# A Mamba-2 mixer with one decay matrix for both directions, and a reordered front, in a two-stream trunk layer

## The chip, the cores and the metric

The kernel runs on one core of a Trainium2 chip. The metric is the device time of one execution in microseconds. The engines are named as the profile names them: PE (TensorE), DVE (VectorE), ACT (ScalarE), POOL (GpSimd) and SP (the engine whose queue issues most of the DMAs; ACT's queue issues some).

## The reference

One layer of a hybrid trunk is computed for 256 context tokens and 1024 latent tokens, with a model width of 1024, all in float32:

```python
shift1, scale1, gate1, shift2, scale2, gate2 = split(silu(c) @ ada_w + ada_b, 6)
h = rmsnorm(x, norm1_g) * (1 + scale1) + shift1
proj = h @ w_in
y_ssd = ssd_mixer(proj[..., :OFF_SGU]);  y_sgu = sgu_mixer(...);  y_s5 = s5_mixer(...)
x = x + gate1 * (concatenate([y_ssd, y_sgu, y_s5]) @ w_out)
h = rmsnorm(x, norm2_g) * (1 + scale2) + shift2
x = x + gate2 * (square(relu(h @ ffn_w1)) @ ffn_w2)
...
# SSD, in each of two directions, per chunk of 128 tokens and head (the backward one on flipped tokens):
seg = a_cum[q] - a_cum[k];  lmat = exp(where(lower, seg, -inf))
y_diag = (C B^T * lmat) @ (x * dt)
chunk_state = B^T @ (decay_to_end * dt * x);  h = chunk_decay * h + chunk_state
y_off = (C @ h_prev) * exp(a_cum)
y = y_f + flip(y_b) + D * x
```

A final rmsnorm follows. The S5 mixer is a complex diagonal scan over 16 groups of 64 states, and the gating mixer (SGU) works on blocks of 128 tokens.

## The kernel before

Matrix products keep float32 accuracy by splitting each operand into a high and a low part and adding three products (`mm3`, lines 219 to 221). Most activations stand with channels on partitions and tokens along the free axis. The tokens are held as three tiles of 256, 512 and 512 columns (`hi[t]`, `lo[t]`), and the first norm works on five blocks of 256 tokens.

The program is written as one long sequence; the order in which each engine really gets its instructions is made by a planner, which simulates the program and puts instructions of later parts into gaps of earlier ones. Each engine, and each queue that issues DMAs, then works strictly in that order. Tiles come from rings with a fixed number of buffers (`bufs`), and a tile waits until the one that used its buffer last has been read.

The part of the program ahead of the second norm, which we call the front, runs in this order:

- The modulation that the first norm needs (`ada_norm1`, four column groups of `ada_w`), the S5 tables (`s5_tables`, mostly small POOL and DVE work), and the weights of the first projections.
- Per block of 256 tokens: load x by channels (`x_block`), `x_stats` (four ACT squares, POOL sums in pairs, then eight matmuls against a column of ones, line 200, the square root and reciprocal, a broadcast by two matmuls, line 205, and an ACT copy `r` to SBUF, line 267), then `x_norm`: for each of eight channel groups one DVE scale `x<-x,gs,r`, one ACT shift that also rounds to `hi`, and one DVE `lo`.
- `vdt` (value half of the SGU and the time steps) per 128 tokens, `s5_in_tile` per token tile, and `s5_prep` for eight pairs of S5 groups, which makes tables on POOL and DVE, transposes and multiplies some on PE, and stores them to DRAM on ACT's queue. `s5_in_store` writes the S5 inputs to `u5_d` with 16 DMAs on the same queue, and `s5_taps` writes its filter taps with eight DMAs for each half.
- `sgu_mix`, then `s5_main` for eight pairs of groups: it reads u, M, Y, XT and Et back on SP's queue, two scans on DVE, products on POOL.
- Four `xbc_slab`s (projection, depthwise convolution, SiLU), `dt_chain`, and two `u_slab`s.
- The SSD (`ssd_group`, twice, for four heads each). For each of ten chunks `outputs()` loads the rows of cumulated decay `rb` (broadcast to all partitions, 512 KB), makes one matrix exp(min(...)) in `rb[:, 1]`, multiplies it by C·B under either triangular mask (line 886: `rb[:, 0]` on DVE, `rb[:, 1]` on POOL), makes `xd`, x times dt for both directions, and adds in PSUM: D times x through a diagonal matrix `diagd` (line 893) and, for both directions and four heads, `xd` times `rb` (line 896). The state's share `po` (line 903) is scaled and added behind it. `new_state` carries the state on.
- In the loops over chunks stand also the other 64 steps of the modulation (`adaln`, line 170: each loads 256 KB of `ada_w` and does four small matmuls), the z slabs, `s5_glu`, and the gathering of mixed outputs (`mixed_tile`) with the first output slabs.

Then come the output projection, the second norm and the feed-forward part, which fill the rest of the time and which the diff does not touch.

## Time and profile before

| | |
|---|---|
| runs | 1589.42, 1590.81, 1593.71 us; median 1590.81 us |
| the profiled execution | 1586.03 us, span from first to last instruction 1584.2 us |
| mean granted TensorE clock | 0.954 of 2.4 GHz |
| busy share of the span | PE 92%, DVE 68%, ACT 46%, POOL 28% |
| matmuls | 8664 records (a float32 matmul that is not split leaves two) |
| first feed-forward matmul | near 708 us |

The span is the time between the first and the last instruction in one execution; the profiled execution's own time is 1.8 us more than its span. Busy times are sums of the recorded durations with overlaps counted once. Matmuls overlap in the pipeline, so the record of one can be longer than the time that it takes from the next.

### The profile page before, as it was taken

To read this page: it belongs to the slowest core of one execution; us is meant where nothing else is said; L and a number is where in the kernel's file an instruction comes from. 1 tells how busy PE (TensorE), PEld (TensorE's weight loads), DVE (VectorE), ACT (ScalarE), POOL (GpSimd) and SP (SyncE) were. 2 spreads that over 40 slices of the span, in tenths; PEclk is the share of its full clock that TensorE was granted. 3 is DMA by queue.
4 is the path that set the end of the run, shared out by engine and by line. 5 is a ranking of instruction groups with operands and counts; after the bars stand their busy time and mean duration, and the time that the engine had idled before them with its cause. 6 is when DMAs were issued, how large, how long until landed. Compare 5 with 4: busy or idle time off the path is not lost.

```text
span 1584.2 us, 24203 instructions
## 1 busy us (share of the span) xinstructions
PE 1459.8 (92%) x8664; PEld 1226.9 (77%) x8664; DVE 1075.9 (68%) x1807; ACT 723.0 (46%) x1428; POOL 447.5 (28%) x537
## 2 busy tenths in 40 slices
PE   4789988999897889989999999999899999999895
PEld 4677877877674668878888888888788988887795
DVE  5885587575755665558977765674554768979945
ACT  3565534463533533436655554455646333424322
POOL 4875376624333331321100000000240313032023
PEclk9699999999997889999999999999999999999897
DMA  9414546368778677446444443444844245415302
GB/s 325 141 68 135 179 149 192 86 182 216 208 261 210 204 246 235 121 123 192 130 156 150 149 141 116 137 140 141 264 132 161 67 160 171 123 54 180 113 34 100
DMA packets 238808, 249.12 MB, mean 157 GB/s; under 512 B 15808, under 2 KB 165344, under 8 KB 238688
## 3 DMA queue, kind: packets, MB, share of 16 engines
q1 hardware_dynamic: 222592, 230.32, 46.9%
q10 hardware_dynamic: 16096, 17.27, 3.2%
q8 instruction: 68, 1.11, 0.3%
q14 instruction: 52, 0.43, 0.1%
HBM read 178.63 MB, written 68.89 MB: 156 GB/s over the span
## 4 chain that ended last, share of the span: by engine, by line
PE 59%; DVE 8%; DMA 6%; issue 2%; ACT 2%; POOL 1%; SPq 0%; DVEq 0%; ACTq 0%; POOLq 0%
PE ps_w L1193 7%; PE ps_w L1194 7%; PE ps_w L1192 7%; PE ps_w L1349 6%; PE ps_w L1348 6%; PE ps_w L1350 6%; PE ps_mm L221 4%; PE ps_mm L219 4%; PE ps_mm L220 4%; DMA xc<-xbc_d 2%; DVE X L54 2%; PE ps_mm L1350 1%; PE ps_mm L1349 1%; PE ps_mm L1348 1%; DMA rb<-rows_d 1%
## 5 line engine op out<-in xcount | busy, mean ns | idle before, releaser
L219 PE MATMUL ps_mm<-hi,wh 128*128 128x512 f32 (+1 forms) x576 | 211.8, 368 | 6.4 <-DVE dtr L686 2.8
L221 PE MATMUL ps_mm<-hi,wl 128*128 128x512 f32 (+1 forms) x576 | 209.4, 364 | 0.9 <-DVE wl L54 0.9
L220 PE MATMUL ps_mm<-lo,wh 128*128 128x512 f32 (+1 forms) x576 | 209.8, 364 | 0.2 <-DVE lo L54 0.2
L1348 PE MATMUL ps_w<-uB,uA 128*128 128x512 f32 (+1 forms) x520 | 190.7, 371 | 9.3 <-ACT uB L60 8.9
L1349 PE MATMUL ps_w<-uB,uA 128*128 128x512 f32 (+1 forms) x520 | 191.7, 369 | 7.7 <-DVE uB L54 7.7
L1350 PE MATMUL ps_w<-uB,uA 128*128 128x512 f32 (+1 forms) x520 | 190.5, 367 | 0.0
L54 POOL TENSOR_TENSOR cb<-h 128x512 f32<-128x512 f32 x14 | 21.1, 1512 | 512.5 <-DMA h<-w 402.7
L219 PEld LDWEIGHTS ps_mm<-hi,wh 128*128 128x128 f32 x576 | 111.2, 193 | 24.7 <-DVE dtr L686 3.2
L221 PEld LDWEIGHTS ps_mm<-hi,wl 128*128 128x128 f32 x576 | 110.9, 193 | 19.1 <-issue 2.4
L220 PEld LDWEIGHTS ps_mm<-lo,wh 128*128 128x128 f32 x576 | 111.1, 193 | 15.9 <-issue 1.2
L1348 PEld LDWEIGHTS ps_w<-uB,uA 128*128 128x128 f32 x520 | 99.9, 193 | 25.4 <-ACT uB L60 9.3
L1349 PEld LDWEIGHTS ps_w<-uB,uA 128*128 128x128 f32 x520 | 100.1, 192 | 24.5 <-DVE uB L54 9.6
L1350 PEld LDWEIGHTS ps_w<-uB,uA 128*128 128x128 f32 x520 | 100.0, 192 | 15.4
L54 DVE TENSOR_TENSOR uB<-tb,uB 128x512 fp32r<-128x512 f32 x106 | 88.7, 857 | 13.5 <-ACT uB L60 13.5
L60 ACT ACTIVATE uB<-tb 128x512 fp32r<-128x512 f32 x106 | 65.6, 625 | 62.1 <-PE ps_w L1350 31.7
L54 DVE TENSOR_TENSOR wl<-wraw,wh 128x1024 fp32r<-128x1024 f32 x32 | 50.3, 1572 | 40.6 <-ACT wh L60 40.2
L54 DVE TENSOR_TENSOR X<-X,ps_w 128x512 f32<-128x512 f32 x84 | 56.1, 680 | 27.7 <-PE ps_w L1350 27.6
L54 DVE TENSOR_TENSOR q<-q,ps_w 128x512 f32<-128x512 f32 x48 | 32.9, 686 | 60.2 <-PE ps_w L1194 59.5
L60 ACT ACTIVATE c<-c 128x512 f32<-128x512 f32 x64 | 40.3, 629 | 56.9 <-DVE c L54 55.9
L54 POOL TENSOR_TENSOR sq<-sq 128x512 f32<-128x512 f32 (+1 forms) x31 | 41.1, 1331 | 81.8 <-ACT sq L60 81.3
L1350 PE MATMUL ps_mm<-ch,uA 128*128 128x256 f32 x224 | 63.2, 283 | 0.0
L1349 PE MATMUL ps_mm<-cl,uA 128*128 128x256 f32 x224 | 63.2, 283 | 0.0
(430 smaller groups left out, 3993.9 us busy)
## 6 DMA issues: line engine op xcount, KB each, us to landing
rw<-w SPq DMA_DIRECT2D x112, 256.0 KB
tb<-a_d SPq DMA_DIRECT2D x106, 256.0 KB
aw<-ada_w SPq DMA_DIRECT2D x64, 256.0 KB
h<-w SPq DMA_DIRECT2D x32, 512.0 KB
a_d<-t SPq DMA_DIRECT2D x42, 256.0 KB
rb<-rows_d SPq DMA_DIRECT2D x20, 512.0 KB
adaw<-ada_w SPq DMA_DIRECT2D x32, 256.0 KB
wraw<-w_out SPq DMA_DIRECT2D x16, 512.0 KB
```

Source lines behind the costliest of these rows:

```text
L54: eng.tensor_tensor(out=out, in0=a, in1=b, op=op)
L60: S.activation(out=out, in_=in_, func=func, **kw)
L219: T.matmul(out, lhsT=wh(k), rhs=xh(k), start=(k == 0), stop=False)
L220: T.matmul(out, lhsT=wh(k), rhs=xl(k), start=False, stop=False)
L221: T.matmul(out, lhsT=wl(k), rhs=xh(k), start=False, stop=(k == nk - 1))
L1192: T.matmul(out, lhsT=wh, rhs=X[0][:, j, :], start=(j == 0), stop=False)
L1193: T.matmul(out, lhsT=wh, rhs=X[1][:, j, :], start=False, stop=False)
L1194: T.matmul(out, lhsT=wl, rhs=X[0][:, j, :], start=False, stop=(j == 3))
L1348: T.matmul(out, lhsT=wh, rhs=bh, start=start, stop=False)
L1349: T.matmul(out, lhsT=wh, rhs=bl, start=False, stop=False)
L1350: T.matmul(out, lhsT=wl, rhs=bh, start=False, stop=stop)
```

## The change

Four things are altered.

- **The SSD chunk.** The two masked products are combined into one matrix, since both directions share C·B and exp(min(...)): for each head, ACT writes `cm[:, 0]` times dt of the forward direction into `rb[:, 0]`, DVE adds `cm[:, 1]` times dt of the backward one, and a single DVE product makes `rb[:, 1]`. The matmul with x itself (`xs`, an ACT copy) then covers both directions: four matmuls instead of eight. D times x leaves PE (`diagd` goes away) and becomes two DVE instructions with `dcol`. `wdec` is multiplied by dt for both directions, so that `new_state` can start from x in PSUM, on DVE for both. The ring of `xc` gets five buffers instead of three.
- **Squares by tokens.** For blocks 1 to 4, `x_rms` replaces `x_stats`: it loads the same x a second time with tokens on partitions (a new input array `xN`, four DMAs of 256 KB a block), lets ACT's squares add up along the row, and leaves the broadcast factor in PSUM, where `x_norm` reads it.
- **Order.** `s5_prep`, in steps, moves from between the norms to between the projections; the two `u_slab`s move ahead of the last steps of it; the 64 modulation steps move from the SSD loops to the projections (five groups of eight) and to `s5_main` (three groups), with their tiles in the common ring `ev`.
- **S5 arrays in DRAM.** `u5_d`, `y5_d` and `kt_d` are stored by channel. The writes of u and of the taps become one DMA in place of eight, the reads in `s5_glu` one in place of eight; the reads and the write of `s5_main` (u2, M, y2) become two in place of one.

```diff
     m5_d = dram.tile([256, NT], F32, name="m5_d")
-    u5_d = dram.tile([16, 8, 16, JP], F32, name="u5_d")
-    y5_d = dram.tile([16, 8, 16, 161], F32, name="y5_d")
-    kt_d = dram.tile([16, 8, 16, 128], F32, name="kt_d")
+    u5_d = dram.tile([256, 8, JP], F32, name="u5_d")
+    y5_d = dram.tile([256, 8, 161], F32, name="y5_d")
+    kt_d = dram.tile([256, 8, 128], F32, name="kt_d")
     yc_d = dram.tile([8, 128, 576], F32, name="yc_d")
...
         return r
+    def x_rms(i):
+        t, o = BLK[i]
+        c0 = TILES[t][0] + o
+        ss = cst.tile([128, 2, 2], F32, tag="ss", name="ss", bufs=2)
+        for j in range(2):
+            for a in range(2):
+                xn = ev("xn")
+                load(xn, I["xN"][c0 + j * 128:c0 + (j + 1) * 128, a * 512:(a + 1) * 512])
+                act(xn, xn, ACT.Square, accum_out=ss[:, j, a:a + 1])
+        rt = cst.tile([128, 4], F32, tag="rt", name="rt", bufs=3)[:, 0:2]
+        tt(rt, ss[:, :, 0], ss[:, :, 1], ALU.add)
+        rstd(rt, rt, D)
+        p = bank("w", 5)
+        for j in range(2):
+            T.matmul(p[:, j * 128:(j + 1) * 128], lhsT=rt[:, j:j + 1].to_broadcast([128, 128]), rhs=ident,
+                     start=True, stop=True)
+        return p[:, 0:256]
...
         tt(kt[:, 112:128], kt[:, 112:128], pk[:, 240:256], ALU.add)
-        for tau in range(8):
-            load(kt_d[hf * 8:(hf + 1) * 8, tau].rearrange("g c n -> g c n"), kt[:, (7 - tau) * 16:(7 - tau) * 16 + 128], nc.scalar)
+        win = bass.AP(kt.tensor, kt.offset + 112, [kt.ap[0], [-16, 8], [1, 128]])
+        load(kt_d[hf * 128:(hf + 1) * 128], win, nc.scalar)
...
     def s5_in_store(m, us):
-        for tau in range(8):
-            load(u5_d[m * 8:(m + 1) * 8, tau], us[:, tau, :], nc.scalar)
+        load(u5_d[m * 128:(m + 1) * 128], us, nc.scalar)
...
         u2 = pool.tile([128, 2, JP], F32, tag="u2", name="u2", bufs=3)
-        load(u2, u5_d[gp * 2:gp * 2 + 2].rearrange("g t c j -> (t c) g j"))
+        gs = [slice((gp * 2 + i) * 16, (gp * 2 + i + 1) * 16) for i in range(2)]
+        for i in range(2):
+            load(u2[:, i, :], u5_d[gs[i]].rearrange("c t j -> t c j"))
         M = pool.tile([128, 2, 128], F32, tag="M", name="M", bufs=3)
-        load(M, kt_d[gp * 2:gp * 2 + 2].rearrange("g t c n -> (t c) g n"))
+        for i in range(2):
+            load(M[:, i, :], kt_d[gs[i]].rearrange("c t n -> t c n"))
         Y = pool.tile([128, 2, 2, 9, 16], F32, tag="Y", name="Y", bufs=3)
...
             stt(y2[:, par, :], u2[:, par, 1:162], s5dd[:, gp * 2 + par:gp * 2 + par + 1], o, ALU.mult, ALU.add)
-        load(y5_d[gp * 2:gp * 2 + 2].rearrange("g t c j -> (t c) g j"), y2)
+        for i in range(2):
+            load(y5_d[gs[i]].rearrange("c t j -> t c j"), y2[:, i, :])
...
             y = cvt("yf", [128, 8, 161])
-            for g in range(8):
-                load(y[g * 16:(g + 1) * 16], y5_d[k * 8 + g].rearrange("t c j -> c t j"))
+            load(y, y5_d[k * 128:(k + 1) * 128])
             act(y, y, ACT.Gelu_apprx_tanh)
...
         act(wdec.rearrange("p d c -> p (d c)"), pc[:, 160:320], ACT.Exp)
-        tt(wdec[:, 1], wdec[:, 1], DTD[:, 1], ALU.mult)
+        tt(wdec, wdec, DTD, ALU.mult)
         act(dtot.rearrange("p d c -> p (d c)"), pc[:, 320:480], ACT.Exp)
...
             o = xoff(c)
-            xc = pool.tile([128, 4, 128], F32, tag="xc", name="xc", bufs=3)[:, 0:n]
+            xc = pool.tile([128, 4, 128], F32, tag="xc", name="xc", bufs=5)[:, 0:n]
             load(xc, xbc_d[g, 0:n, :, o:o + 128].rearrange("a p n -> p a n"))
...
             xw = pool.tile([128, 4, 64], F32, tag="xw", name="xw", bufs=2)
-            tt(xw, px, scal(wdec, d, c).unsqueeze(2).to_broadcast([128, 4, 64]), ALU.mult, V if d else G)
+            tt(xw, px, scal(wdec, d, c).unsqueeze(2).to_broadcast([128, 4, 64]), ALU.mult)
             pst = bank("ws")[:, 0:256]
...
                 tt(cm, pcb.unsqueeze(1).to_broadcast([128, 2, 128]), tri[:, 0:2], ALU.mult)
-                for d, E in ((0, V), (1, G)):
-                    tt(rb[:, d], rb[:, 1], cm[:, d].unsqueeze(1).to_broadcast([128, 4, 128]), ALU.mult, E)
-                xd = pool.tile([128, 2, 4, 64], F32, tag="xd", name="xd", bufs=2)
-                tt(xd, px.unsqueeze(1).to_broadcast([128, 2, 4, 64]),
-                   DTD[:, :, c * 8 + g * 4:c * 8 + g * 4 + 4].unsqueeze(3).to_broadcast([128, 2, 4, 64]), ALU.mult)
+                d0, d1 = scal(DTD, 0, c), scal(DTD, 1, c)
+                for hh in range(4):
+                    act(rb[:, 0, hh], cm[:, 0], ACT.Copy, scale=d0[:, hh:hh + 1])
+                    stt(rb[:, 0, hh], cm[:, 1], d1[:, hh:hh + 1], rb[:, 0, hh], ALU.mult, ALU.add)
+                tt(rb[:, 1], rb[:, 1], rb[:, 0], ALU.mult)
+                xs = pool.tile([128, 4, 64], F32, tag="xs", name="xs", bufs=2)
+                S.copy(xs, px)
                 py = bank("wb", 2)[:, 0:256].rearrange("p (a q) -> p a q", a=2)
                 for a in range(2):
-                    T.matmul(py[:, a, :], lhsT=diagd[:, 2 * g + a, :], rhs=xc[:, a], start=True, stop=False)
-                    for d in range(2):
-                        for par in range(2):
-                            T.matmul(py[par * 64:(par + 1) * 64, a, :], lhsT=xd[:, d, 2 * a + par],
-                                     rhs=rb[:, d, 2 * a + par], start=False, stop=(d == 1))
+                    for par in range(2):
+                        T.matmul(py[par * 64:(par + 1) * 64, a, :], lhsT=xs[:, 2 * a + par], rhs=rb[:, 1, 2 * a + par],
+                                 start=True, stop=True)
                 hs_ = (hf, hb[c])
...
                 tt(er[:, ds], po[:, ds], er[:, ds], ALU.mult)
-                tt(cm, er[:, dirs[0]], py, ALU.add)
+                for a in range(2):
+                    stt(cm[:, a], xc[:, a], dcol[:, 2 * g + a:2 * g + a + 1], py[:, a], ALU.mult, ALU.add)
                 if len(dirs) == 2:
-                    tt(cm, cm, er[:, 1], ALU.add, G)
+                    tt(er[:, 0], er[:, 0], er[:, 1], ALU.add, G)
+                tt(cm, cm, er[:, dirs[0]], ALU.add)
                 load(y_d[g * 256:(g + 1) * 256].rearrange("(a p) n -> p a n", p=128)[:, :, c * 128:(c + 1) * 128], cm)
                 if c < NCH - 1:
-                    hf = new_state("hf", 2, 0, c, xd[:, 0], bt, hf, "hf")
+                    hf = new_state("hf", 2, 0, c, px, bt, hf, "hf")
                 yield
...
         x_norm(0, r, range(4, KD))
-        x_block(1, px)
-        x_block(2, px)
+        rs = {}
+        for i in (1, 2):
+            rs[i] = x_rms(i)
+            x_block(i, px)
         w5 = [wslab(I["w_in"][:, 2064 + m * 128:2192 + m * 128], nc.scalar) for m in range(2)]
         us = [s5_in_start(m) for m in range(2)]
-        x_block(3, px)
-        x_block(4, px)
         load(pk2, I["pk2"])
         prep = s5_prep_all(p5w, R5)
-        rs = {i: x_stats(i) for i in (1, 2)}
         for i in range(1, 5):
+            if i > 1:
+                rs[i + 1] = x_rms(i + 1) if i < 4 else None
+                if i < 4:
+                    x_block(i + 1, px)
             x_norm(i, rs[i])
-            if i > 1:
-                next(prep)
-            if i < 3:
-                rs[i + 2] = x_stats(i + 2)
+        ada = (x for q in range(4, 12) for x in adaln(q, lambda: ev("aw"), 512))
+        def ada_group():
+            for _ in range(8):
+                next(ada, None)
         for i in range(5):
...
                     s5_in_tile(i // 2, w5[m], us[m])
+            ada_group()
+            next(prep, None)
         for m in range(2):
...
         V.tensor_scalar(out=glubh, in0=glub, scalar1=0.5, scalar2=None, op0=ALU.mult)
+        sgu_mix()
+        for m in range(2):
+            u_slab(m)
         for _ in prep:
             pass
-        sgu_mix()
     with tc.tile_pool(name="p5m", bufs=1) as p5m:
...
         for gp in range(8):
+            if gp in (0, 2, 4):
+                ada_group()
             cur = s5_main(p5m, gp, s5zm)
...
     dt_chain()
-    for m in range(2):
-        u_slab(m)
     psA.close()
     with tc.tile_pool(name="pd", bufs=1) as pd, banks("psB"):
-        diagd = pd.tile([128, 4, 128], F32, name="diagd")
-        for i in range(4):
-            G.tensor_scalar(out=diagd[:, i], in0=ident, scalar1=dcol[:, i:i + 1], scalar2=None, op0=ALU.mult)
         (right0, out0), (right1, out1) = [ssd_group(pd, g) for g in range(2)]
-        ada = (x for q in range(4, 12) for x in adaln(q, lambda: pd.tile([128, 512], F32, tag="aw", name="aw", bufs=2), 512))
-        def step(n):
-            for _ in range(n):
-                next(ada, None)
         def drain(g):
...
         for c, _ in enumerate(out0):
-            step(3)
             if c >= 5:
...
                     out_slab(m, (0,), wo[m])
-            step(4)
             if c in (2, 6):
                 mixed_tile(c // 4)
-        step(64)
         stt(gs2, mod[:, 32:40, :], 1.0, g2.unsqueeze(2).to_broadcast([128, 8, 2]), ALU.add, ALU.mult)
...
         xT=np.concatenate([f["x_prompt"][0], f["x_sample"][0]], axis=0).T,
+        xN=np.concatenate([f["x_prompt"][0], f["x_sample"][0]], axis=0),
         pk1=pack(PK1), pk2=pack(PK2), pk3=pack(PK3),
```

## Rows read from the trace of the kernel before

**Rows 1.** Busy per stretch: times, length, PE, PEld, DVE, ACT, POOL, clock, DMA share, GB/s.

```profile
57.00:147.00 90.00, 77.15 (x478) 68.48 (x476) 69.14 (x123) 57.64 (x137) 65.93 (x86) 0.90 0.25 88
147.00:194.00 47.00, 41.82 (x278) 35.08 (x277) 28.48 (x57) 21.23 (x41) 18.25 (x33) 0.96 0.59 175
194.00:313.00 119.00, 110.10 (x630) 92.61 (x629) 90.31 (x137) 46.20 (x111) 76.80 (x105) 0.96 0.49 148
313.00:460.00 147.00, 137.91 (x944) 106.19 (x943) 93.76 (x154) 71.31 (x142) 53.36 (x57) 0.99 0.74 219
460.00:580.00 120.00, 102.60 (x791) 71.25 (x793) 73.36 (x155) 50.98 (x117) 44.65 (x49) 0.83 0.75 215
```

**Rows 2.** Timeline of DVE: start, length, instruction, times, idle before.

```profile
57.71 7.53 DVE L57 SCALAR_TENSOR_TENSOR x<-x,gs,r 128x256 f32<-128x256 f32 x8 [0.63 <-ACT r L267]
...
79.50 8.38 DVE L57 SCALAR_TENSOR_TENSOR x<-x,gs,r 128x256 f32<-128x256 f32 x8
...
101.82 8.24 DVE L57 SCALAR_TENSOR_TENSOR x<-x,gs,r 128x256 f32<-128x256 f32 x8 [0.61 <-ACT r L267]
...
119.95 3.26 DVE L57 SCALAR_TENSOR_TENSOR x<-x,gs,r 128x256 f32<-128x256 f32 x8 [4.31 <-ACT r L267]
```

**Rows 3.** Busy time per stretch, of the third and fourth block's scales.

```profile
101.80:110.10 8.30, 5.65 (x26) 4.34 (x24) 8.28 (x10) 5.88 (x14) 7.50 (x7) 1.00 0.13 50
119.90:123.30 3.40, 3.40 (x29) 3.40 (x29) 3.35 (x9) 3.40 (x16) 0.00 (x0) 1.00 0.01 2
```

**Rows 4.** Groups of instructions to 720 us: busy, mean ns; a scale from PSUM.

```profile
L57 DVE SCALAR_TENSOR_TENSOR acc<-acc,gs,ps_ad 128x256 f32<-128x256 f32 x4 | 1.6, 466 | 0.0
```

**Rows 5.** Timeline of ACT and of its DMA queue.

```profile
41.41 2.19 ACT L60 ACTIVATE sq<-x 128x512 f32<-128x512 f32 x4 [3.41 <-POOL eh L54]
...
147.42 12.09 ACTq L48 DMA_DIRECT2D u_d<-us  x11
160.39 1.76 ACT L465 COPY yz<-Y 64x288 f32<-64x288 f32 x4 [12.36 <-DMA u_d<-us]
...
184.11 3.39 ACTq L48 DMA_DIRECT2D kt_d<-kt  x5
```

**Rows 6.** Timeline of SP's queue: the first read of S5 inputs.

```profile
189.40 0.37 SPq L48 DMA_DIRECT2D u<-u_d  x1
```

**Rows 7.** Groups on PE to 720 us.

```profile
L896 PE MATMUL ps_wb<-rb,xd 128*64 128x128 f32 x320 | 33.6, 317 | 2.3 <-DVE rb L54 2.1 <-POOL rb L54 0.2
...
L170 PE MATMUL ps_ad<-aw,sc 128*32 128x128 f32 x512 | 28.8, 303 | 7.4 <-DMA aw<-ada_w 4.7 <-DVE mod L54 2.7
...
L893 PE MATMUL ps_wb<-xc,diagd 128*128 128x128 f32 x80 | 20.2, 338 | 0.6 <-DVE er L54 0.6
...
L200 PE MATMUL ps_ad<-ones,sq 128*128 128x1 f32 x108 | 17.4, 280 | 15.7 <-POOL sq L54 15.7
```

**Rows 8.** Groups of the SSD chunk on DVE, POOL, ACT, and one beside it.

```profile
L57 DVE SCALAR_TENSOR_TENSOR rb<-rb,col 128x128 f32<-128x128 f32 x80 | 34.9, 474 | 16.2 <-ACT rb L60 16.0
...
L60 ACT ACTIVATE rb<-rb,col 128x128 f32<-128x128 f32 x80 | 26.2, 391 | 0.4
L54 POOL TENSOR_TENSOR rb<-rb,cm 128x512 f32<-128x512 f32 x20 | 25.6, 1281 | 9.8 <-DVE rb L54 4.0 <-ACT rb L60 2.0 <-DMA wraw<-w_out 1.1
...
L54 DVE TENSOR_TENSOR rb<-rb,cm 128x512 f32<-128x512 f32 x20 | 18.8, 941 | 0.0
...
L54 DVE TENSOR_TENSOR xd<-ps_wa,DTD 128x512 f32<-128x512 f32 x20 | 13.6, 679 | 0.0
...
L54 DVE TENSOR_TENSOR cm<-er,ps_wb 128x256 f32<-128x256 f32 x20 | 8.2, 412 | 3.2 <-PE ps_wb L896 3.1
...
L57 DVE SCALAR_TENSOR_TENSOR vq<-ps_mm,pk,sgub 128x128 f32<-128x128 f32 x20 | 5.7, 344 | 3.7 <-PE ps_mm L700 2.8 <-DMA mix_d<-vq 0.9
```

**Rows 9.** Waits from 313 to 580 us: who, for whom, us in total, times, longest.

```profile
SPq L48 <- PE ps_ad L170: 21.2, 23, 4.4
...
ACT er L60 <- DMA rb<-rows_d: 37.2, 12, 6.4
```

## The prediction

> **What bounds the kernel now.** The page comes first: PE is busy 92% of the span and DVE 68%, as in the table above, which says where to look and not yet what binds. Then the part that the diff touches is cut into stretches [rows 1]. From 57 to 147 us (norms, first projections) PE is idle for 12.9 of 90 us and its clock is at 0.90; the timeline of DVE shows why: three blocks of eight scales take 7.53, 8.38 and 8.24 us, and the fourth 3.26 [rows 2]. During the third POOL is busy for 7.50 of 8.30 us, during the fourth not at all [rows 3]. DVE paces that stretch, because its instructions with both operands in SBUF are slowed while POOL works. From 147 to 313 PE is busy 151.9 of 166 us. In the SSD, 313 to 580, PE is busy 240.5 of 267 us, DVE 167.1, ACT 122.3, POOL 98.0, and from 460 on the granted clock is at 0.83, so part of PE's time there is time at 1.2 GHz. The waits of the SSD show SP's queue standing 21.2 us for PE to free modulation tiles, and ACT waiting 37.2 us for the decay rows that the same queue issues [rows 9].
>
> **The change, part by part.** The sum is made against the profiled execution's 1586.03 us, 4.8 us under the median of the runs, 1590.81; the difference is added again at the end.
>
> Norms. The factor r now comes from PSUM. A scale of 256 columns from PSUM takes 466 ns, the undisturbed one from SBUF 3.26/8 = 408 [rows 2, 4]. The 24 slow scales take 24.15 us now; at 0.41 to 0.47 they take 9.8 to 11.2, which frees DVE of 13 to 14 us. The rows show the slowdown beside POOL and its absence without [rows 2, 3]. The Trainium skill (SBUF — State Buffer, section "Who interferes with whom") states the same as a rule: a DVE instruction with two SBUF inputs shares a read port with POOL and one of them stops, one with a single SBUF input does not. By that rule the PSUM scales are free of POOL however busy it is, which would give the full 14 us.
>
> Four blocks lose eight matmuls against the ones each, two records a matmul: 64 of the 108 records, 17.4 × 64/108 = 10.3 us of PE, some 8 of them behind 57 us [rows 7]. POOL loses eight sums. What comes is hidden: four squares a block stay on ACT, their sums are tiny. The 1 MB of x by tokens is queued on SP ahead of each block; blocks 1 and 2 gain 2 MB. At the 88 GB/s that this stretch moves there is room; ahead of it x of block 1 had landed when its squares began at 41.41 [rows 5], 16 us before its scale at 57.71, and 2 MB at the SSD's 219 GB/s are 9.6 us [rows 1, 2], so the cover holds. Without it the start slips by those 9.6 us.
>
> Tables and stores. ACT's queue issues eleven stores of u for 12.09 us, and the next ACT instruction, a copy that the tables need, starts after 12.36 us of waiting; five stores of taps take 3.39, so eight take some 5.4 [rows 5]. One store in place of eight leaves one or two us. The S5 loads start at 189.40 [rows 6], behind both. But PE is filled meanwhile by slabs (41.8 of 47 us), so this 14 us is not a gain by itself; it lets S5 start earlier, and the u slabs cover the tables' end in their new place. `s5_main` pays 24 more DMAs on SP at 0.37 us, 9 us over 119 us; queued behind them are the next pair's loads, three pairs ahead.
>
> Modulation. Its 512 records are 28.8 us of PE, 3.6 a group, moved whole from the SSD to the front [rows 7], with 64 loads of 256 KB. In the front SP is mostly free and DMA 25% to 59% busy [rows 1]. The tiles come from a ring shared with xn, so a load can stand in SP's queue until PE is through; behind it wait weights and S5 loads.
>
> Front in sum, 57 to 313 us: PE busy 229.1 of 256, less 8, plus 28.8, is 250, which would fit with 6 us to spare. The stretch at clock 0.90 gives back up to 7 if the gaps go: 243. With every gap filled that is −13, and with the tables also done by idle engines and the clock whole −19. If half of the 26.9 us of gaps stay, 250 + 13 is +7. I take −9, near the end at which DVE's 14 us are PE's gaps, because the two stand in the same 90 us.
>
> The SSD chunk. PE loses the diagonal's 20.2 us and half of the 33.6 [rows 7], 37.0, and of the modulation 26: 240.5 becomes 178. DVE loses `xd` 13.6 and one sum 8.2; the product with `rb` stays one. It gains 80 adds of 128 columns at 0.344 (a like one from PSUM) to 0.474 (mean of those beside POOL), 27.5 to 37.9; 40 instructions for D times x at 0.344, 13.8; 20 sums and 18 products of 256 columns at 0.412, 15.7 [rows 8]. Net +35 to +46. POOL loses the products of `rb`, 25.6 us, and those of `xw`; if that freed DVE wholly, the old 80 would drop from 474 to 344 ns, 10.4 us, and the `rb` product from 941 to the 679 of `xd`, 5.2. So DVE goes from 167.1 to between 187 and 213; I take 200. ACT gains 80 scales at 391 ns and 20 copies, some 38: 160, not the bound. SP loses its 21 us of waits for the modulation.
>
> How long is a stretch in which DVE needs 200 and PE 178? At PE's present share, 0.90, and the low bound of DVE it is 187/0.90 = 208, −59; at DVE's share in 194 to 313, 0.76 [rows 1], and the high bound, 213/0.76 = 280, +13. I take 200/0.83 = 241, midway between the shares: −26.
>
> Sum: −9 − 26 = −35, so 1551 for the profiled execution and 1556 for the median. What follows 580 us is unchanged and starts earlier.
>
> **The rivals.** (a) *A larger gain*: the clock of the second SSD group returns to full and the stretch keeps PE's share with DVE at 195: 195/0.90 = 217, −50, front −13: 1528. For it, 0.83 of clock over 120 us; against it, DVE as dense as PE is now.
>
> (b) *PE's busy time was never the bound in the SSD*, and the order of dependent steps is. Weight loads there are busy 177.4 of 267 us, 66% [rows 1]. Then removed matmuls win little, and what counts is the decay rows coming earlier: about a third of ACT's 37.2 us, −12, front 0: 1579. The Trainium skill (Perfetto Trace Analysis, section "Identifying the Most-Contended Engine") holds that matmul busy share is a poor measure of headroom and weight-load share a better one. By that rule this rival would be the forecast; the gaps of PE in [rows 1] are few, which speaks against it.
>
> (c) *The front does not take the modulation*: PE keeps its gaps, SP stands before ring tiles, +7, and the SSD gives −24: 1574.
>
> (d) *Slower: DVE becomes the bound of the SSD at a poor share.* Its new steps lie in a row (mask, four adds after four ACT scales, product, then PE, then D times x, then the sum), and each engine works in order. With 200 us of work, the stretch may last 276 before the front's 9 us are used up: the point is a share of 0.72. At 0.68, 294 us, it is +27 − 9 = +18: 1609. DVE's share today is 0.63 here with PE as the bound, 0.76 where it works with POOL in S5.
>
> **How the numbers follow.** Forecast 0.52, (a) 0.20, (b) 0.12, (c) 0.06, (d) 0.10. About 0.3%, 5 us, is what a measurement of this kernel can tell from no change. The forecast's own span is 1540 to 1575. The range takes in (a), (b) and (c) and leaves out (d) and the far ends: 1520 to 1588. Faster: 0.52 + 0.20 + 0.05 of (c) + 0.07 of (b) = 0.84; same: 0.05 of (b) and 0.01 of (c) = 0.06; slower 0.10.
>
> **What would show it.** The eight scales of blocks 1 to 3 at 3.3 to 3.8 us each time; no gap of 12 us on ACT; S5's first load before 180 us; 250 us of PE in the front with PE above 95%; in the SSD, PE near 178 and DVE near 200 busy, its stretch near 241 us. I am wrong if DVE's share in the SSD stays below 0.72, if PE's gaps in the front are as long as now, or if the planner lays the stretches out so differently that neither is to be found.

## The result, and the profile after

The changed kernel takes 1578.73 us (median; 1577.43 to 1582.45), the kernel before 1590.12 in the same comparison: a ratio of 0.9935, 95% interval 0.9911 to 0.9959. It is faster by 11 us, outside the 0.3% that count as no change, but by a third of the 35 us forecast, and 1578.73 is far from 1556, though inside the range. The profiled execution has a span of 1576.7 us (before 1584.2).

The stretches of [rows 1], now of the changed kernel, in the same columns; the last line reaches from 57 us to the first output slab's sum, which we take as the end of the SSD (581.0 us; before 585.4):

```profile
57.00:147.00 90.00, 76.16 (x655) 63.06 (x656) 51.77 (x109) 40.59 (x105) 42.21 (x62) 0.91 0.65 210
147.00:194.00 47.00, 38.91 (x307) 30.18 (x306) 20.65 (x55) 21.14 (x56) 24.44 (x42) 0.89 0.78 217
194.00:313.00 119.00, 110.97 (x780) 89.19 (x779) 84.34 (x148) 47.59 (x119) 77.73 (x105) 0.97 0.58 184
313.00:460.00 147.00, 132.89 (x722) 108.11 (x721) 103.29 (x190) 85.63 (x173) 30.20 (x34) 0.97 0.63 175
460.00:580.00 120.00, 84.52 (x420) 66.18 (x419) 91.95 (x239) 77.10 (x197) 23.61 (x31) 0.76 0.59 157
57.00:581.00 524.00, 444.44 (x2887) 357.72 (x2888) 353.01 (x740) 273.02 (x650) 198.18 (x274) 0.90 0.62 182
```

The same line of the kernel before, from 57 us to the end of its SSD:

```profile
57.00:585.40 528.40, 473.65 (x3155) 377.29 (x3154) 359.63 (x632) 251.26 (x552) 258.99 (x329) 0.93 0.59 176
```

Here one sees where the gain went. PE is busy for 29.2 us less (473.65 to 444.44), and idle for 24.8 us more (54.8 to 79.6). What was taken from PE came back as gaps, most of them in the last stretch: 84.5 busy of 120, at a granted clock of 0.76.

The norms and the stores did what was forecast. Timeline of DVE, to be held against [rows 2]:

```profile
47.00 2.82 DVE L57 SCALAR_TENSOR_TENSOR x<-x,gs,ps_w 128x256 f32<-128x256 f32 x7
...
70.06 3.22 DVE L57 SCALAR_TENSOR_TENSOR x<-x,gs,ps_w 128x256 f32<-128x256 f32 x8 [3.10 <-PE ps_w L285]
...
82.64 5.97 DVE L57 SCALAR_TENSOR_TENSOR x<-x,gs,ps_w 128x256 f32<-128x256 f32 x15 [3.84 <-PE ps_w L285]
```

Busy time in the first of these three, POOL in the column after ACT:

```profile
47.00:49.82 2.82, 1.27 (x4) 0.95 (x4) 2.82 (x10) 2.78 (x7) 2.76 (x6) 0.50 1.09 358
```

Timeline of ACT's DMA queue, against [rows 5]; then of POOL, and of SP's queue against [rows 6]:

```profile
142.69 0.57 ACTq L48 DMA_DIRECT2D u_d<-us  x1
...
149.77 0.52 ACTq L48 DMA_DIRECT2D u_d<-us  x1
...
176.00 0.53 ACTq L48 DMA_DIRECT2D kt_d<-kt  x1
```

```profile
150.71 0.10 POOL L806 MEMSET xr<- 128x2 f32 x1 [9.87 <-DMA u_d<-us]
```

```profile
183.98 1.39 SPq L48 DMA_DIRECT2D u<-u_d  x2
```

The scales take 0.40 us each instead of one, and the last `lo` of the norms starts at 107.4 us (126.0 before). ACT's queue is free. But POOL stands 9.87 us for the same store: the planner put the clearing of an `xr` tile, whose ring buffer the store still reads, ahead of table work. The kernel before has the like, 5.08 us for that store and 7.58 for another:

```profile
155.49 0.10 POOL L785 MEMSET xr<- 128x2 f32 x1 [5.08 <-DMA u_d<-us]
...
163.25 0.10 POOL L785 MEMSET xr<- 128x2 f32 x1 [7.58 <-DMA et_d<-Et]
```

The SSD's first transpose stands at 324.4 us, 8.6 later than before (315.8), and its end 13 us nearer to that start (256.6 us; before 269.6). But the loops over chunks are no shorter. Their products with x (line 896 before, 918 now; the view gives the first and the last start) reach over 199.8 us in both kernels, and the busy times of just these stretches, before and after, show less work on PE, more on DVE and the same length:

```profile
L896 PE MATMUL ps_wb<-rb,xd x320: 272/273/477, 376.5 to 576.3; 128*64 128x128 f32 x160
L918 PE MATMUL ps_wb<-rb,xs x160: 272/323/476, 389.7 to 589.5; 128*64 128x128 f32 x160
```

```profile
376.50:576.30 199.80, 177.02 (x1346) 125.44 (x1347) 123.61 (x256) 86.45 (x200) 73.38 (x83) 0.90 0.77 227
389.70:589.50 199.80, 153.05 (x807) 119.66 (x806) 146.99 (x374) 122.79 (x300) 35.95 (x46) 0.83 0.64 175
```

What PE did in the front, groups from 57 to 313 us: the high part of the slab and S5 projections, and the modulation; the third line is the first one's like in the kernel before, where the modulation was not there:

```profile
L219 PE MATMUL ps_mm<-hi,wh 128*128 128x512 f32 (+1 forms) x203 | 75.0, 369 | 16.0 <-DVE dtr L707 16.0
...
L170 PE MATMUL ps_ad<-aw,sc 128*32 128x128 f32 x512 | 22.9, 290 | 1.8 <-DMA aw<-ada_w 1.8
```

```profile
L219 PE MATMUL ps_mm<-hi,wh 128*128 128x512 f32 (+1 forms) x238 | 88.4, 372 | 4.3 <-DVE dtr L686 2.8 <-ACT xr L791 0.8 <-DVE vq L57 0.8
```

Each such matmul has two companions (lines 220 and 221), so we speak of triples: 35 fewer stand in the front, at 372 + 369 + 368 ns about 39 us. They went to the SSD, and its loops took in others from behind: after the last product with x stand 167 triples instead of 192, and from there to the first feed-forward matmul (702.4 us; before 707.7) it takes 112.9 us instead of 131.4. Groups of the changed kernel from 324 to 581 us, against [rows 7, 8]:

```profile
L57 DVE SCALAR_TENSOR_TENSOR rb<-rb,col 128x128 f32<-128x128 f32 x80 | 27.2, 380 | 17.0 <-ACT rb L60 17.0
L854 PE MATMUL ps_ws<-xw,bt 128*128 128x256 f32 x72 | 27.0, 461 | 29.5 <-DVE xw L54 23.4 <-DMA z<-z_d 2.8 <-DMA xc<-xbc_d 2.5
...
L57 DVE SCALAR_TENSOR_TENSOR rb<-cm,DTD,rb 128x128 f32<-128x128 f32 x80 | 25.9, 369 | 4.2 <-ACT rb L60 4.2
L60 ACT ACTIVATE rb<-cm,DTD 128x128 f32<-128x128 f32 x80 | 25.4, 390 | 4.5 <-DVE cm L54 4.4
...
L918 PE MATMUL ps_wb<-rb,xs 128*64 128x128 f32 x150 | 16.7, 357 | 0.4 <-PE ps_wa L845 0.2 <-DVE rb L54 0.2
L54 DVE TENSOR_TENSOR rb<-rb 128x512 f32<-128x512 f32 x20 | 15.4, 772 | 0.0
...
L57 DVE SCALAR_TENSOR_TENSOR cm<-xc,pk,ps_wb 128x128 f32<-128x128 f32 x36 | 10.8, 340 | 2.3 <-PE ps_wb L918 2.2
...
L54 DVE TENSOR_TENSOR cm<-cm,er 128x256 f32<-128x256 f32 x18 | 10.3, 572 | 1.8 <-POOL er L54 1.8
```

PE now waits 29.5 us ahead of the state's matmul (line 854), 23.4 of it for `xw`, whose forward half moved from POOL to DVE and stands there behind the chunk's other steps. Ahead of the same matmul it waited 6.2 us before.

### The profile page after: what moved, and what is told of

Read it like the earlier page. It is cut to its first block, busy times and chain, and to the rows that moved or that the text cites. A ratio compares the mean times of both kernels' runs of the same rounds, so it can differ in the third digit from the quotient of the medians.

```text
span 1576.7 us, 23817 instructions
## 1 busy us (share of the span) xinstructions
PE 1423.4 (90%) x8360; PEld 1202.6 (76%) x8360; DVE 1067.9 (68%) x1929; ACT 751.1 (48%) x1541; POOL 389.5 (25%) x487
## 4 chain that ended last, share of the span: by engine, by line
PE 58%; DVE 8%; DMA 6%; ACT 2%; issue 2%; POOL 1%; SPq 0%; DVEq 0%; ACTq 0%; POOLq 0%
PE ps_w L1215 7%; PE ps_w L1213 7%; PE ps_w L1214 7%; PE ps_w L1369 6%; PE ps_w L1370 6%; PE ps_w L1371 6%; PE ps_mm L219 4%; PE ps_mm L221 4%; PE ps_mm L220 4%; DMA rb<-rows_d 2%; PE ps_mm L1371 1%; PE ps_mm L1370 1%; PE ps_mm L1369 1%; DVE X L54 1%; DVE rb L57 1%
## 5 line engine op out<-in xcount | busy, mean ns | idle before, releaser
L219 PEld LDWEIGHTS ps_mm<-hi,wh 128*128 128x128 f32 x576 | 111.2, 193 | 38.1 <-DVE dtr L707 16.8
L1371 PE MATMUL ps_mm<-ch,uA 128*128 128x256 f32 x224 | 63.2, 283 | 0.0
L1369 PE MATMUL ps_mm<-ch,uA 128*128 128x256 f32 x224 | 63.1, 283 | 0.0
```

Of the source, the lines that this page charges most:

```text
L219: T.matmul(out, lhsT=wh(k), rhs=xh(k), start=(k == 0), stop=False)
L1369: T.matmul(out, lhsT=wh, rhs=bh, start=start, stop=False)
L1371: T.matmul(out, lhsT=wl, rhs=bh, start=False, stop=stop)
```

## The experiments

The theory after the result was that the parts of the change carry each other, and that something other than PE's work paces the SSD: the loads of decay rows on SP's queue (first theory), or the chain of dependent steps (its rival). All were timed beside the kernel before; times are medians of several runs, ratios are to the kernel before. A difference from the changed kernel is worked out from two such ratios, so it is good to some 5 us.

### Parts alone, on the kernel before

**e1: the SSD chunk alone.** In the kernel before:

```diff
-                for d, E in ((0, V), (1, G)):
-                    tt(rb[:, d], rb[:, 1], cm[:, d].unsqueeze(1).to_broadcast([128, 4, 128]), ALU.mult, E)
+                for hh in range(4):
+                    act(rb[:, 0, hh], cm[:, 0], ACT.Copy, scale=d0[:, hh:hh + 1])
+                    stt(rb[:, 0, hh], cm[:, 1], d1[:, hh:hh + 1], rb[:, 0, hh], ALU.mult, ALU.add)
+                tt(rb[:, 1], rb[:, 1], rb[:, 0], ALU.mult)
...
```

> The kernel before with the SSD chunk of the change alone (one decay matrix, D times x on DVE, new_state from PSUM; xc stays at three buffers, the modulation stays in the SSD loops, the front is the old one). Theory 1 (the loops over chunks are paced by the loads of decay rows and x, B, C that stand on SP's queue, not by PE or DVE): the 37 us of PE that go away leave the stretch from the first to the last chunk's product near its 200 us, and the time within 5 us of the kernel before. Rival (PE's work was the bound, and the modulation's move spoiled the result elsewhere): 20 us faster or more. Second rival (DVE's longer row of steps is the bound): slower by 5 us or more.

1595.76 us, ratio 1.0039 (1.0019 to 1.0058). The SSD got 7 us longer (276.7) although 37 us of PE's matmuls left it, so less work for PE does not shorten it by itself. By the expectation this is the second rival, DVE's longer row of steps. The waits from 313 to 600 us name something else besides: PE stands 25.8 us for the modulation's loads, for 4.7 in [rows 7]. The run doesn't separate the two.

```profile
PE ps_ad L170 <- DMA aw<-ada_w: 25.8, 12, 5.9
```

**e2: the squares by tokens alone.**

```diff
-        rs = {i: x_stats(i) for i in (1, 2)}
+        rs = {i: x_rms(i) for i in (1, 2)}
...
-                rs[i + 2] = x_stats(i + 2)
+                rs[i + 2] = x_rms(i + 2)
...
```

> The kernel before with squares by tokens alone for blocks 1 to 4 (r stays in PSUM). Theory 1 (the norms paced the stretch from 57 to 147 us, and what the change saved there was filled up with modulation matmuls): scales of 256 columns at 0.40 us, the norms end some 15 us earlier, the SSD starts 8 to 15 us earlier, and the time is 8 to 15 us below the kernel before. Rival (PE's own work from 57 to 313 us is the bound whatever the norms do): the norms end earlier and the time stays within 4 us.

1607.38 us, ratio 1.0113 (1.0082 to 1.0144), against both expectations. The norms end 14 us earlier (111.8), and nothing comes of it: from 57 to 147 us PE is busy for 65.1 us instead of 77.2, and 213 triples stand ahead of 313 us instead of 238. Up to there PE waits 10.2 us for the new factor itself:

```profile
L285 PE MATMUL ps_w<-pk,rt 128*128 128x128 f32 x15 | 3.1, 353 | 10.2 <-DVE rt L190 10.2
```

**e10: S5's layout in DRAM alone.**

```diff
-    u5_d = dram.tile([16, 8, 16, JP], F32, name="u5_d")
+    u5_d = dram.tile([256, 8, JP], F32, name="u5_d")
...
-        for tau in range(8):
-            load(u5_d[m * 8:(m + 1) * 8, tau], us[:, tau, :], nc.scalar)
+        load(u5_d[m * 128:(m + 1) * 128], us, nc.scalar)
...
```

> The kernel before with one part of the change: S5's u, y and table arrays in DRAM with one store from ACT's queue each, and two loads and stores on SP's queue for a pair of blocks. Put back to the old layout, the changed kernel lost 23 us. If that gain belongs to the layout itself (12 us of stores leave ACT's queue and S5's groups start earlier): 1567 to 1582 us. If it belongs to the changed front, where the S5 tables stand last and nothing else covers them, and the kernel before has cover (projections beside them): 1583 to 1593 us.

1595.16 us, ratio 1.0033 (1.0012 to 1.0053), later than either expectation. S5 begins 8 us earlier (186.7) and ends 6 earlier, but again with 213 triples ahead of 313 us, and the SSD is 9 us longer.

**e5: the modulation alone**, beside each pair of dt projections and ahead of S5's pairs 0, 2 and 4.

```diff
+            ada_group()
...
-            step(3)
...
-            step(4)
...
-        step(64)
```

> The kernel before with one part of the change: the 64 steps of the modulation leave the SSD loops and stand as in the change (eight steps beside each pair of dt projections, eight ahead of S5 main's groups 0, 2 and 4). The SSD chunk, the norms' squares and S5's tables stay as they were. If moving the modulation is what made the change faster (it was worth 19 us between the changed kernel and the one with the steps put back): 1570 to 1578 us, 11 to 19 below the kernel before, the SSD about 12 us shorter and the front 4 us or less longer. If the moved modulation pays only together with the lighter chunk, since the old chunk leaves PE with 240 us of work in a stretch of 267: 1585 to 1592 us.

1633.07 us, ratio 1.0265 (1.0241 to 1.0288): 42 us slower, against both expectations. The stretch 147 to 194 us of this kernel:

```profile
147.00:194.00 47.00, 27.66 (x285) 15.78 (x283) 7.73 (x13) 13.37 (x34) 24.14 (x42) 0.70 0.92 285
```

The DMAs are at 0.92 and 285 GB/s, and PE is idle for 19 us; in its waits from 57 to 200 us stands

```profile
PE ps_ad L170 <- DMA aw<-ada_w: 13.1, 12, 3.3
```

The steps start at 128.2 us here, 77.9 in the changed kernel. Their 16.8 MB then meet S5's start, and only 137 triples stand ahead of 313 us.

**e6: modulation and chunk**, the edits of e1 and e5 together.

```diff
+            ada_group()
...
-            step(3)
...
+                tt(rb[:, 1], rb[:, 1], rb[:, 0], ALU.mult)
...
```

> The kernel before with two parts of the change: the modulation moved to the front and the new SSD chunk; norms, u slabs and S5's layout as before. With the runs of each part alone it fills a square of four. If the parts add up: mod alone plus 7 us, since the chunk alone was 6.7 us slower than the kernel before. If PE's busy time bounds the SSD as soon as the modulation is gone, the lighter chunk now pays: some 10 us below mod alone, 1560 to 1568 us. If loads and stores on SP's queue set the SSD's pace, the chunk is worth nothing here either: within 7 us of mod alone.

1627.74 us, ratio 1.0231 (1.0208 to 1.0254), 5 us below e5, which is within the 7 us of the third expectation; the two intervals overlap. So with the modulation gone the chunk costs nothing here, where by itself it cost 7.

**e8: as e6, four buffers for the rows.**

```diff
-                rb = pool.tile([128, 2, 4, 128], F32, tag="rb", name="rb", bufs=3)
+                rb = pool.tile([128, 2, 4, 128], F32, tag="rb", name="rb", bufs=4)
```

> As the kernel with the modulation moved and the new chunk (norms, u slabs and S5 as before), with four buffers in place of three for the decay rows. If the loads of the decay rows, which wait for a free buffer on SP's in-order queue, pace the SSD: 5 us or more below the kernel with three buffers, as the changed kernel gained 5 us from the fourth. If another wait paces it: within 3 us of it.

1624.34 us, ratio 1.0208 (1.0182 to 1.0234): 3 us, which the intervals don't tell from nothing.

### Parts taken out of the change

**e3: the modulation put back** into the SSD's loops, all else changed.

```diff
-            ada_group()
...
+            step(3)
...
+            step(4)
...
+        step(64)
```

> The changed kernel with the 64 modulation steps put back into the loops over chunks, everything else as changed. Theory 1: the front loses 29 us of PE work, so the SSD starts 10 to 20 us earlier than in the changed kernel; the SSD, which PE does not bound, grows by 10 us or less; the time is 5 to 15 us below the changed kernel. Rival (moving the modulation is what made the change faster): 5 to 15 us above the changed kernel, with SP's queue again standing about 20 us for modulation tiles.

1598.06 us, ratio 1.0063 (1.0039 to 1.0087): the move is worth 20 us here, more than the rival expected, where alone it cost 42. Without it 225 triples stand ahead of 313 us instead of 203, and the SSD starts 4 us earlier (320.2), but from 313 to 600 us PE waits 33.6 us for the modulation's loads, which cost it 1.8 in the front above:

```profile
PE ps_ad L170 <- DMA aw<-ada_w: 33.6, 16, 6.3
```

**e9: the old chunk** in the changed kernel.

```diff
-                tt(rb[:, 1], rb[:, 1], rb[:, 0], ALU.mult)
+                for d, E in ((0, V), (1, G)):
+                    tt(rb[:, d], rb[:, 1], cm[:, d].unsqueeze(1).to_broadcast([128, 4, 128]), ALU.mult, E)
...
```

> The changed kernel with the SSD chunk of the kernel before (two decay matrices, D times x on TensorE by diagonal matrices, three buffers for the chunk's columns); front, S5's layout and the moved modulation as changed. In the kernel before the new chunk cost 6.7 us by itself, and with the modulation moved it gained 5 us. If TensorE's busy time sets the SSD's pace once the modulation is gone: about 60 us of TensorE come back, and the time is 1590 us or more. If the chain of dependent steps and loads sets it: within 8 us of the changed kernel, 1571 to 1587 us.

1592.02 us, ratio 1.0007 (0.9988 to 1.0026): 11 us more than the changed kernel. By its time this is the expectation for PE (1590 us or more), but only 22.6 us of PE's work come back, not 60. To the end of its SSD (589.4) PE is busy for 467.0 us and idle for 65.4. The new chunk saves 22.6 us of PE and 14.2 of them return as gaps. So PE's work has some weight in the changed kernel; how much isn't shown, since DVE's and POOL's work and the buffers of `xc` change with it.

**e7: the old layout of S5** in the changed kernel, the edit of e10 reversed.

```diff
-        load(u5_d[m * 128:(m + 1) * 128], us, nc.scalar)
+        for tau in range(8):
+            load(u5_d[m * 8:(m + 1) * 8, tau], us[:, tau, :], nc.scalar)
...
-        for i in range(2):
-            load(u2[:, i, :], u5_d[gs[i]].rearrange("c t j -> t c j"))
+        load(u2, u5_d[gp * 2:gp * 2 + 2].rearrange("g t c j -> (t c) g j"))
...
```

> The changed kernel with S5's u, y and table arrays in DRAM laid out as before: eight stores each from ACT's queue again, and one load each of u and M and one store of y for a pair of blocks on SP's queue. If the 24 more issues on SP's queue are what made S5 main longer (125 us from its first to its last matmul, 114 before): S5 main 113 to 117 us, the SSD starts near 315 us, and the time is 1569 to 1574 us, less what the long ACT stores cost (12 us on ACT's queue). If S5 main is longer because the modulation's matmuls and the order of the slabs stand in it: S5 main stays near 125 us, and the time is 1577 to 1585 us.

1601.68 us, ratio 1.0065 (1.0045 to 1.0085): the layout is worth 21 us here, more than either expectation has, and cost 5 alone. S5 begins at 207.6 us (192.0). It is about as long as in the changed kernel (122 and 125 us), so the 24 more DMAs on SP's queue don't make it longer. The stretch 147 to 194 us:

```profile
147.00:194.00 47.00, 25.27 (x220) 18.78 (x219) 26.68 (x55) 15.57 (x46) 20.73 (x37) 0.67 0.57 168
```

**e11: the old squares** in the changed kernel.

```diff
-            rs[i] = x_rms(i)
             x_block(i, px)
+            rs[i] = x_stats(i)
...
```

> The changed kernel with the norms' squares of blocks 1 to 4 summed as before (squares on ACT, adds on POOL, column sums on TensorE, the scale row copied to SBUF); everything else, the order included, as changed. In the kernel before the squares by tokens alone cost 18 us though the norms ended 14 us earlier. If the earlier norms are what lets the modulation start at 78 us and spread its 13 MB of loads: the norms end near 120 us, the front is 8 us or more longer, and the time is 1585 to 1600 us. If the squares by tokens are worth nothing here either, since their loads stand on SP's queue ahead of the modulation's: 1570 to 1580 us.

1613.19 us, ratio 1.0142 (1.0109 to 1.0174): 33 us more than the changed kernel, and above both expectations. The norms end near 128 us, the modulation starts at 123.2, and the stretch 147 to 194 us looks like that of e5, DMAs at 0.97 and PE idle for 21 us:

```profile
147.00:194.00 47.00, 25.97 (x270) 15.11 (x269) 12.10 (x39) 15.82 (x46) 15.10 (x30) 0.60 0.97 278
```

**The eight together.** Triples ahead of 313 us, and PE's idle time from 57 us to the end of the SSD:

| kernel | ratio | triples | PE idle, us |
|---|---|---|---|
| before | 1 | 238 | 54.8 |
| changed | 0.9935 | 203 | 79.6 |
| chunk alone / taken out | 1.0039 / 1.0007 | 233 / 201 | 82.6 / 65.4 |
| squares alone / taken out | 1.0113 / 1.0142 | 213 / 158 | 77.3 / 91.8 |
| S5 layout alone / taken out | 1.0033 / 1.0065 | 213 / 185 | 63.0 / 101.3 |
| modulation alone / taken out | 1.0265 / 1.0063 | 137 / 225 | 91.8 / 92.3 |

Alone the parts add up to +71 us; together, with the new places of the u slabs and of `s5_prep`, which were not tried by themselves, they are −11. How much of the difference those two places make is open. Each part alone lengthens PE's idle time, by 8 to 37 us.

### What paces the SSD

**e4: four buffers for the decay rows** in the changed kernel.

```diff
-                rb = pool.tile([128, 2, 4, 128], F32, tag="rb", name="rb", bufs=3)
+                rb = pool.tile([128, 2, 4, 128], F32, tag="rb", name="rb", bufs=4)
```

> The changed kernel with four buffers for the decay rows instead of three. If the loops over chunks wait for these loads (theory 1), a load can be issued a chunk earlier, ACT's waits for it fall by a third or more, and the time falls by 4 to 12 us. If DVE or PE pace the loops, nothing changes beyond 3 us.

1573.89 us, ratio 0.9904 (0.9878 to 0.9930), the best of all, some 5 us under the changed kernel; the two intervals overlap. ACT's wait for the rows from 324 to 580 us falls from 28.8 to 4.9 us, far more than the third that was expected, and the products with x (line 918) reach over 190.7 us instead of 199.8. So the rows' lateness has a part in the length of the loops, and some 5 us of it in the time.

```profile
ACT er L60 <- DMA rb<-rows_d: 28.8, 10, 5.3
ACT er L60 <- DMA rb<-rows_d: 4.9, 1, 4.9
```

The first line is the changed kernel's, the second that of e4.

**e12: four buffers, and `xw` of the forward state on POOL.**

```diff
-            tt(xw, px, scal(wdec, d, c).unsqueeze(2).to_broadcast([128, 4, 64]), ALU.mult)
+            tt(xw, px, scal(wdec, d, c).unsqueeze(2).to_broadcast([128, 4, 64]), ALU.mult, E)
...
-                    hf = new_state("hf", 2, 0, c, px, bt, hf, "hf")
+                    hf = new_state("hf", 2, 0, c, xs, bt, hf, "hf", G)
...
```

> The changed kernel with four buffers for the decay rows and with the forward state's weighting of x (20 of 36, 0.47 us each) on POOL, from the copy of x in SBUF, in place of VectorE from PSUM. In the SSD TensorE waits 23 us for VectorE's weighted x in the changed kernel. If VectorE's order in the chunk is what TensorE waits for: 5 us or more below the kernel with four buffers alone (1574), 1562 to 1569 us. If the loads pace the SSD, or POOL's two-input work slows VectorE by as much: 1571 to 1580 us.

1581.9 us, ratio 0.995 (0.9931 to 0.997): 7 us slower than e4. From 324 to 580 us PE's wait for `xw` (27.2 us in e4) is gone, and one nearly as long has come at the transposes, whose PSUM tile the copy `xs` still reads:

```profile
PE ps_wa L845 <- ACT xs L914: 21.1, 10, 8.2
```

The edit also puts that copy ahead of `xw`, and POOL stands for it:

```profile
POOL xw L54 <- ACT xs L914: 38.2, 12, 7.5
```

Still the loops got shorter: the products with x reach over 181.8 us, for 190.7 in e4. The time did not follow. Behind the last product stand 184 triples instead of e4's 167, and the first feed-forward matmul starts at 706.1 us instead of 698.0.

**e14: each load of rows twice.**

```diff
                 load(rb, rows_d[:, c * 8 + g * 4:c * 8 + g * 4 + 4, :].partition_broadcast(128))
+                load(rb, rows_d[:, c * 8 + g * 4:c * 8 + g * 4 + 4, :].partition_broadcast(128))
```

> The changed kernel with every load of decay rows (20 of 512 KB) issued twice into the same buffer; the second is not needed. If the transfers of the rows pace the SSD (5 to 10 us from issue to landing, eight to ten of them on the chain that ends last): each chunk waits 3 to 6 us longer, 40 us or more in all, 1620 us or later. If the steps on the engines pace it and the loads run ahead: 1578 to 1590 us.

1622.17 us, ratio 1.0193 (1.0165 to 1.0221), and an SSD of 300.5 us for 256.6. By the expectation the rows pace the SSD. But a doubled load shows only that twice the load would pace it.

**e17: half of each load.** The backward decay is left out: its rows aren't loaded, and the forward ones are read in their place.

```diff
-                load(rb, rows_d[:, c * 8 + g * 4:c * 8 + g * 4 + 4, :].partition_broadcast(128))
+                load(rb[:, 0], rows_d[0, c * 8 + g * 4:c * 8 + g * 4 + 4, :].partition_broadcast(128))
...
```

> The changed kernel, where each load of decay rows brings only the forward direction's rows (256 KB for 512 KB), and the instructions that read the backward rows read the forward ones; the backward decay is thus left out. All engines keep their instructions. If the transfer of the rows sets the SSD's pace in the changed kernel, as a doubled one does at 2.2 us for each of 20: half of it gives back 10 to 20 us, 1558 to 1569 us. If doubling only brought the loads up to the chain of steps, which paces the SSD in the changed kernel: 1572 to 1580 us.

1577.81 us, ratio 0.9919 (0.9902 to 0.9937): not told from the changed kernel. With 5.2 MB (half of 20 loads) out of the stretch, PE's wait for `xw` from 324 to 580 us is longer than the 23.4 us of the changed kernel:

```profile
PE ps_ws L854 <- DVE xw L54: 33.1, 7, 13.0
```

ACT's wait for the rows is as long as the 28.8 us of the changed kernel:

```profile
ACT rb L60 <- DMA rb<-rows_d: 28.1, 11, 5.2
```

So the size of the transfer is not what makes the rows late, and halving it doesn't test what their lateness costs; e4 does. The products with x reach over 189.3 us here, 10 less than in the changed kernel, and again the time hardly follows. As what sets the time, the transfer of the rows falls; their lateness keeps the 5 us of e4, and the chain of steps stays.

**e15: the rows from POOL's queue.**

```diff
-                load(rb, rows_d[:, c * 8 + g * 4:c * 8 + g * 4 + 4, :].partition_broadcast(128))
+                load(rb, rows_d[:, c * 8 + g * 4:c * 8 + g * 4 + 4, :].partition_broadcast(128), nc.gpsimd)
```

> The changed kernel with the loads of the decay rows issued from POOL's queue in place of SP's. If their place behind stores and loads that wait on SP's in-order queue is what makes them late: as much as the fourth buffer gave (5 us) or more, 1565 to 1574 us. If they are late because their buffer comes free late, or the transfer takes its time: 1575 to 1585 us, more if POOL's own work waits behind the issue.

1590.78 us, ratio 0.9993 (0.9977 to 1.001): 9 us slower than the changed kernel. POOL itself now stands for the buffer, and its own work behind it; waits from 324 to 580 us:

```profile
POOL rb L48 <- PE ps_wb L918: 26.2, 8, 8.6
```

**e16: 16 modulation steps in the second group's loop.**

```diff
-        ada = (x for q in range(4, 12) for x in adaln(q, lambda: ev("aw"), 512))
+        ada = (x for q in range(4, 10) for x in adaln(q, lambda: ev("aw"), 512))
...
         for c, _ in enumerate(out1):
+            next(ada2, None)
+            next(ada2, None)
...
```

> The changed kernel with the last 16 of the 64 modulation steps (two of the eight groups, 7 us of TensorE at the rate of the kernel before) taken out of S5 main and put into the second SSD group's loop, two for each chunk, with two buffers of their own. In the changed kernel TensorE stands idle for 35 us of 460 to 600 and its clock falls to 0.76. If these gaps are free for filling: S5 main ends 5 us or more earlier, the SSD gets no longer, 1568 to 1575 us. If the steps displace what the chunks wait for, as all 64 did (20 us for 64): 5 us more than the changed kernel, 1580 to 1588 us.

1588.47 us, ratio 0.998 (0.9962 to 0.9998): 7 us slower than the changed kernel. S5 ends no earlier (320.6; 317.3), and the SSD is 9 us longer. PE's gaps there are not free to fill, as the second expectation has it.

**e18: five buffers for the rows, three for the columns.**

```diff
-            xc = pool.tile([128, 4, 128], F32, tag="xc", name="xc", bufs=5)[:, 0:n]
+            xc = pool.tile([128, 4, 128], F32, tag="xc", name="xc", bufs=3)[:, 0:n]
...
-                rb = pool.tile([128, 2, 4, 128], F32, tag="rb", name="rb", bufs=3)
+                rb = pool.tile([128, 2, 4, 128], F32, tag="rb", name="rb", bufs=5)
```

> The changed kernel with five buffers for the decay rows, and three for the chunk's columns in place of five, so that both fit. If the rows' loads pace the SSD and more of them may run ahead: as good as the kernel with four buffers, or better, 1565 to 1574 us. If the columns need their five buffers (the kernel before had three), or four are enough: 1574 to 1583 us.

1577.65 us, ratio 0.9924 (0.99 to 0.9949): as the changed kernel. ACT's wait for the rows is down to 4.6 us from 324 to 580 us, but PE now waits for the columns:

```profile
PE ps_wa L845 <- DMA xc<-xbc_d: 14.3, 8, 5.1
```

**e13: one more memset** in the kernel before, to see whether any edit makes the planner lay out a new order.

```diff
         prep = s5_prep_all(p5w, R5)
+        V.memset(vr, 0.0)
```

> The kernel before with one more instruction: a memset of a 128 by 10 tile on VectorE ahead of S5's preparation, far under 1 us of work, and the tile is written again before it is read. The planner lays the whole order out anew all the same: most instructions of TensorE stand elsewhere. If the order by itself is worth little: within 3 us of the kernel before. If the parts' prices when alone (5 to 18 us) are largely the new order: 5 us or more away from it, on either side.

1592.33 us, ratio 1.0006 (0.9985 to 1.0027). The premise was wrong: the order of all engines stayed as it was but for the memset. So the run doesn't price a new order. It shows something else: in its one profile the SSD starts 6 us later (321.9) with the clock of 57 to 147 us at 0.85 for 0.90, while the medians agree. Milestones of two profiles can differ by that much with no cause in the program.

## Why the prediction was wrong in size

**Norms: right.** The scales from PSUM take 2.82/7, 3.22/8 and 5.97/15 us, 0.40 each (forecast 0.41 to 0.47), and the first seven do so while POOL is busy for 2.76 of 2.82 us. The Trainium skill's rule (SBUF — State Buffer, section "Who interferes with whom"), that an instruction with one SBUF input is free of POOL, agrees with this trace. The norms' last `lo` starts 18.6 us earlier, which is more than the 14 us of DVE.

**Tables and stores: right on ACT, short of its aim.** The 12 us of stores are 1.1, the gap is gone, and the first S5 load stands at 183.98, not before 180. The POOL wait of 9.87 us was not in the forecast, though the kernel before had the like. S5 then takes 125 us from its first to its last matmul instead of 114. It isn't the DMAs on SP (e7: 122) nor the modulation (e3 has none there, and takes 124); what it is stays open.

**Front in sum, −9: wrong, and this step failed first.** It read "PE busy 229.1 of 256, less 8, plus 28.8, is 250, which would fit with 6 us to spare". That took PE's work in the front as given. It isn't: the planner fills S5 with slabs, and what finds no place there goes into the SSD. PE was busy for 226.0 of 256 us, 88% and not above 95%; the modulation took 22.9, and 35 triples, 39 us, were pushed into the SSD. With the modulation put back (e3), 22 of them return. PE's gaps in the front are as long as before, 30.0 us for 26.9, which the prediction named as a sign of being wrong: DVE's 14 us did not become PE's. Waits that were not in the forecast stand in them, 16.0 us for `dtr`, in the line of the slab matmuls above. The SSD started 8.6 us later, where 9 earlier was forecast. One profile's clock can shift this by 6 us (e13), but in eight profiles with the changed front (the changed kernel, e4, e9, e12, e14, e15, e17, e18) the SSD starts at 324.4 to 329.5 us, and in three with the old one (before, e1, e13) at 315.8 to 321.9. In the front it went as rival (c) has it.

**The SSD chunk, −26: wrong in PE and in the share, right in DVE.** DVE is busy for 195.2 us from 313 to 580 (forecast 200). The sums of 256 columns take 572 ns instead of 412; the old `rb` instructions take 380 and 772, between the 474 and 941 of before and the 344 and 679 that the prediction gave a DVE freed of POOL. ACT has 163 (forecast 160). PE has 217.4 instead of 178: 194 triples stand in this stretch, where 152 stood. The term that was mis-sized is the share in 200/0.83. DVE's share of the SSD came out at 188.8 of 256.6 us, 0.74, lower than the 0.76 of S5 that the prediction had as its far bound:

```profile
324.40:581.00 256.60, 207.01 (x1091) 165.51 (x1090) 188.83 (x423) 160.27 (x367) 53.64 (x62) 0.87 0.62 170
```

The SSD up to the first output slab is 13 us shorter, not 26, and its loops are as long as before (199.8 us), with PE busy for 0.77 of them and DVE for 0.74.

**The rivals.** (b) gave 1579 and the time is 1579, but the number is luck: its front of 0 was +8.6 us, and ACT's wait for the rows, a third of which was to go, fell from 37.2 to 28.8 us only. Of its reason a part holds. In the kernel before, 37 us less of PE's matmuls gave no time (e1, +7); in the changed kernel 22.6 us more of PE's work came with 11 us of time (e9), so there PE's work has some weight. The rows' lateness is worth some 5 us (e4), which is not clear of noise. What remains is the chain of dependent steps. That is argued by exclusion, and e4 and e12 bear it out for the loops, which got 9 us shorter with each wait that was taken out. But the time gained 5 us in e4 and lost 7 in e12, so what a shorter chain would give the kernel is open. The Trainium skill (Perfetto Trace Analysis, section "Identifying the Most-Contended Engine"), with weight loads as the better measure of headroom than matmul busy share, was nearer the mark: PE's weight loads are busy for 174.3 of 267 us, 65%, and for 66% before, while PE's matmul time in the loops fell by 24 us and left them as long. (a) and (d) were off: the clock fell instead of rising, and DVE's share, 0.74, stayed just above 0.72.

**What made it faster**, then, is not one part. The early norms let the modulation's steps begin at 77.9 us instead of 123 to 128 (e5, e11), and S5's stores in one piece bring S5 in before PE's work runs out (e7). On that ground the modulation's leaving the SSD is worth 20 us (e3) and the chunk 11 (e9). The new chunk needs the move: where it stands beside the modulation, PE waits 25.8 us (e1) or 33.6 us (e3) for the modulation's loads, with the old chunk 4.7.
